# Queries and keys kept as exact float32r halves, attention scores as three products of halves

## The chip, the cores and the metric

The kernel runs on one core of one Trainium2 chip. The metric is the device time of one execution in microseconds (us); what is compared is the median of several executions. The engines are named as the profile names them: PE (TensorE) multiplies, PEld is its loading of weights, DVE is VectorE, ACT is ScalarE, POOL is GpSimd, and SP issues the DMAs that bring the weights in.

## The reference

Two decoder layers over 256 tokens of width 1024, all in float32. Each layer is a half-step SwiGLU, a mixer and a second half-step SwiGLU. The mixer projects once and runs three branches side by side: a gated causal convolution of 31 taps, a gated spatial mixing, and attention with 8 heads of 64. With 256 tokens and blocks of 256 there is one block, so the attention is plain causal attention:

```python
q = _partial_rope(z_q.reshape(bsz, seq, ATT_HEADS, HEAD_DIM), cos, sin)
k = _partial_rope(z_k.reshape(bsz, seq, ATT_HEADS, HEAD_DIM), cos, sin)
...
s = jnp.einsum("bhqd,bhqnkd->bhqnk", qc, kg).astype(jnp.float32) * scale   # scale = 64 ** -0.5
s = jnp.where(mask, s, -jnp.inf)
p = jax.nn.softmax(...)
return jnp.einsum("bhqnk,bhqnkd->bhqd", p, vg)
```

## The kernel before

Weights come in chunks of 1 MB (128 x 2048). Each chunk is split into two float32r halves: ACT copies the rounded half (`whi`, line 114) and DVE subtracts it from the chunk (`wlo`, line 115), in two pieces of 1024 columns in most stages. Activations are split in the same way, and a product of the two is then three matmuls, high by high, low weight by high, high by low (lines 271 to 273, and 456 to 458 in the sections that put tokens on partitions). A chunk is worked on by 48 such matmuls.

The mixer begins with four blocks of the convolution's gate. Then come four sections: queries, keys, the gating's v, the attention's v. `rotated` (464) scales and turns the queries, then the keys. `columns_first` (483) is run in the middle of the next section: PE transposes the turned queries (or keys) so that head dimensions lie on partitions, and ACT copies them to `qT` (or `kT`), with the factor 1/8 for queries. Through all of this DVE has 124 steps of the convolution to do in its free time (`conv`, 438, lines 442 and 444), some after each stage.

After two more blocks (`uT`) comes the stage that the change touches most. `scores(c)` (545) makes the scores of heads 2c and 2c+1, each head in a PSUM bank of its own: a mask product in bf16 (550), a float32 product for the first 128 queries (552) and one for the others (555). DVE takes the maxima (`st`, 565), ACT the exponentials (line 85 in the profile, the helper `act`), DVE divides (570, 572). `turned(c)` (575) transposes them on PE (580) and copies them with ACT (`aT`, 582), `values(c)` (586) multiplies by v (590, 591) and splits the result into `yc_`. The order on PE is: scores(0), scores(1), half a block of gate weights, `mix` (524: the gating's product, 530), half a block; then for c = 0 to 3: turned(c), half a block, values(c), scores(c+2) while there are any, half a block.

All of this shares one group of four PSUM banks, `acc`: the two banks of a scores(c), the two of mix, the two of a turned(c) and the one of a values(c). A tile that finds no free bank waits until an earlier one has been read out for the last time. Likewise `qT`, `kT`, `yc`, `uT`, the halves of the gating (`yb`) and those of the attention's result (`yc_`) share seven places of 4 KB (tag `b4`).

In the trace each engine takes its instructions in the order in which they stand in its queue. That order, and which buffer a tile gets, is set when the program is built: a scheduler goes through the code by priority and by its own estimate of when things are ready. Of an engine's instructions, one that waits holds up all that stand behind it.

Of the kernel before, what the change touches and what calls it, by code (L numbers as in the profile page):

```python
# [9 lines left out]
F32 = mybir.dt.float32  # L10
F32R = mybir.dt.float32r
BF16 = mybir.dt.bfloat16
AF = mybir.ActivationFunctionType
# [4 lines left out]
P = 128  # L18
D = 1024
S = 256  # L20
# [6 lines left out]
NCW = CW // P  # L27
TAPS = 31
HEADS = 8
HD = 64  # L30
# [16 lines left out]
def decoder_kernel(ctx, tc, x_in, wts, rows, lanes, sguw, rope, out):  # L47
    nc = tc.nc
# [8 lines left out]
    sm = ctx.enter_context(tc.tile_pool(name="sm", bufs=4))  # L57
    ps = ctx.enter_context(tc.tile_pool(name="ps", bufs=4, space=PSUM))

    def bank(tag="ps"):  # L60
        return ps.tile([P, 512], F32, name=tag, tag=tag, bufs=4)
# [4 lines left out]
    TS = [slice(t * P, (t + 1) * P) for t in range(NT)]  # L66
# [50 lines left out]
    def cols(n, i):  # L117
        return slice(i * CH // n, (i + 1) * CH // n)
# [11 lines left out]
    def weights():  # L130
        i = used[0]
        used[0] += 1
        ensure(i + LOOK)
        return made.pop(i)
# [128 lines left out]
    def t2(name):  # L263
        return wk.tile([P, 512], F32, name=name, tag="t2", bufs=12)
# [14 lines left out]
    def pair_block(ph, at_k=None, k_at=KD // 2 - 1, nudged=False):  # L279

        w = blocks(KD)
        b = bank()
        if nudged:
            nudge(b, w[0][:, 0, 0], ph.xh)
        for k in range(KD):
            for s in range(2):
                product(b[:, s * S:(s + 1) * S], w, (slice(None), k, s), (ph.xh, ph.xl), k,
                        k == 0 and s == 0, k == KD - 1 and s == 1)
            if at_k is not None and k == k_at:
                at_k()  # L290
        return b

    def scaled(b, ph, name="t"):

        t = t2(name)
        nc.vector.tensor_mul(two(t), two(b), ph.R.to_broadcast([P, 2, S]))  # L296
        return t
# [99 lines left out]
    def wide(name):  # L397
        return mx.tile([P, NCW, S], F32, name=name, tag="b4", bufs=7)

    def halves4(name):  # L400
        return [mx.tile([P, NCW, S], F32R, name=f"y{name}{k}", tag="b4", bufs=7) for k in "hl"]

    def layer_stats(src):
        bs = sm.tile([P, 6], F32, name="bs", bufs=4)
        nc.vector.bn_stats(bs, src)
        mv = sm.tile([P, 2], F32, name="bmv", bufs=4)
        nc.vector.bn_aggr(mv, bs)
        v = sm.tile([P, 1], F32, name="bv", bufs=4)
        nc.vector.tensor_scalar_add(v, mv[:, 1:2], EPS)
        r = sm.tile([P, 1], F32, name="br", bufs=4)  # L410
        nc.gpsimd.tensor_tensor(r, v, mhalf[:, 0:1], op=OP.pow)
        b = sm.tile([P, 1], F32, name="bb", bufs=4)
        nc.vector.scalar_tensor_tensor(b, mv[:, 0:1], -1.0, r, op0=OP.mult, op1=OP.mult)
        return r, b

    def mixer(l, ph, lane, params, make_next):
# [21 lines left out]
        def conv(n, after=None):  # L438
            for k, c in taps[:n]:
                src, w = yp[:, c, k:k + S], convw[:, c, k:k + 1]  # L440
                if k == 0:
                    ins = nc.vector.tensor_scalar(yc[:, c], src, w, cb[:, c:c + 1], op0=OP.mult, op1=OP.add)
                else:
                    ins = nc.vector.scalar_tensor_tensor(yc[:, c], src, w, yc[:, c], op0=OP.mult, op1=OP.add)  # L444
                behind(ins, after)
            del taps[:n]

        def section(between=None):

            b = [bank() for _ in range(NT)]  # L450
            for c in range(2):
                w = [h.rearrange("p (k m) -> p k m", k=4) for h in weights()]
                for t in range(NT):
                    for kk in range(4):
                        hx, lx = (v[:, 4 * c + kk, TS[t]] for v in x)
                        nc.tensor.matmul(b[t], hx, w[0][:, kk], start=c == 0 and kk == 0, stop=False)  # L456
                        nc.tensor.matmul(b[t], hx, w[1][:, kk], start=False, stop=False)  # L457
                        nc.tensor.matmul(b[t], lx, w[0][:, kk], start=False, stop=c == 1 and kk == 3)  # L458
                if c == 0 and between is not None:
                    between()  # L460
            return b


        def rotated(b):
            zs = []
            for t in range(NT):
                zf = t2("zqk")
                nc.scalar.activation(zf, b[t], AF.Identity, scale=ph.r[:, t:t + 1])
                z = zf.rearrange("p (h d) -> p h d", h=HEADS)
                x12 = z[:, :, :RD]  # L470
                sw = sm.tile([P, HEADS, RD], F32, name="sw", bufs=2)
                hf = RD // 2
                cb_ = rp[:, t, 0:1, :].to_broadcast([P, HEADS, RD])
                sb_ = rp[:, t, 1:2, :].to_broadcast([P, HEADS, RD])
                nc.vector.tensor_mul(sw[:, :, :hf], z[:, :, hf:RD], sb_[:, :, :hf])
                nc.vector.tensor_mul(sw[:, :, hf:], z[:, :, :hf], sb_[:, :, hf:])
                nc.vector.tensor_mul(x12, x12, cb_)
                end = nc.vector.tensor_add(x12, x12, sw)
                zs.append(zf)
            conv(11, end)  # L480
            return zs

        def columns_first(dst, srcs, **kw):
            for t in range(NT):
                pt = bank("acc")
                for c in range(NCW):
                    nc.tensor.transpose(pt[:, c * P:(c + 1) * P], srcs[t][:, c * P:(c + 1) * P], ident)
                nc.scalar.activation(dst[:, :, TS[t]], pt.rearrange("p (c m) -> p c m", c=NCW), AF.Copy,
                                     **kw)

        qT, kT = wide("qT"), wide("kT")
        zq = rotated(section())
        zk = rotated(section(lambda: columns_first(qT, zq, scale=HD ** -0.5)))


        b = section(lambda: columns_first(kT, zk))
        gvs = []
        for t in range(NT):
            gv = t2("gv")
            act(gv, b[t], AF.Gelu_apprx_tanh, scale=ph.r[:, t:t + 1])  # L500
            r, b_ = layer_stats(gv)
# [6 lines left out]
        b = section()  # L508
        vt = []
        for t in range(NT):  # L510
            vv = mx.tile([P, HEADS, HD], F32, name=f"v{t}")
            nc.scalar.activation(vv.rearrange("p h d -> p (h d)"), b[t], AF.Identity,
                                 scale=ph.r[:, t:t + 1])
# [4 lines left out]
        for c in (0, 2):  # L518
            t = scaled(pair_block(ph), ph)
# [25 lines left out]
        def scores(c):  # L545
            heads = (0, 1)
            rows_ = [slice(h * HD, (h + 1) * HD) for h in heads]
            pS = [bank("acc") for _ in heads]
            for h in heads:
                nc.tensor.matmul(pS[h][:, :3 * P], ident_b, causal_b, start=True, stop=False)  # L550
            for h in heads:
                nc.tensor.matmul(pS[h][:, 0:P], qT[rows_[h], c, 0:P], kT[rows_[h], c, 0:P],
                                 start=False, stop=False)
            for h in heads:
                nc.tensor.matmul(pS[h][:, P:3 * P], qT[rows_[h], c, P:S], kT[rows_[h], c, :],
                                 start=False, stop=True)
            ways = (slice(0, P), slice(P, 3 * P))
            res = []
            with tc.high_priority():
                for h in heads:  # L560
                    sc = wk.tile([P, 3 * P], F32, name="sc", bufs=4)
                    st = sm.tile([P, NT], F32, name="st", bufs=4)
                    su = sm.tile([P, NT], F32, name="su", bufs=4)
                    for t, w in enumerate(ways):
                        nc.vector.tensor_reduce(st[:, t:t + 1], pS[h][:, w], axis=AX.X, op=OP.max, negate=True)
                    for t, w in enumerate(ways):
                        act(sc[:, w], pS[h][:, w], AF.Exp, bias=st[:, t:t + 1], accum_out=su[:, t:t + 1])
                    res.append((sc, su))
                for sc, su in res:
                    nc.vector.reciprocal(su, su)  # L570
                    for t, w in enumerate(ways):
                        nc.vector.tensor_scalar_mul(sc[:, w], sc[:, w], su[:, t:t + 1])
            return [sc for sc, _ in res]
# [68 lines left out]
        m = [wide("m") for _ in range(2)]  # L642
# [85 lines left out]
    for i in range(2):  # L728
        nc.scalar.dma_start(xt[:, 4 * i:4 * i + 4], x_in[:, 4 * i:4 * i + 4])
        c = cols(2, i)  # L730
        loaded[0] = nc.sync.dma_start(first[0][:, c], wts[0, :, c])
    ph = Phase(lane[0][:, L_GAIN:L_GAIN + KD])
# [25 lines left out]
    for l in range(DEPTH):  # L758
# [3 lines left out]
        def gains(i, cur=cur):  # L762
            return cur[:, L_GAIN + KD * i:L_GAIN + KD * (i + 1)]
# [5 lines left out]
        ph = ffn(ph, lambda: Phase(gains(1)), lambda: params.extend(mixer_params(l)), 2 if l == 0 else 1)  # L769
        ph = mixer(l, ph, cur, params, lambda: Phase(gains(2)))  # L770
        if l < DEPTH - 1:
            ph = ffn(ph, lambda: Phase(lane[-1][:, L_GAIN:L_GAIN + KD]), following)
# [105 lines left out]
```

## Time and profile before

| | us |
|---|---|
| median of 3 runs (lowest to highest) | 1198.89 (1196.75 to 1201.77) |
| the profiled execution, its own time | 1201.76 |
| its span, first to last instruction | 1200.0 |
| PE busy | 1178.3 (98%) |
| DVE busy | 853.8 (71%) |
| ACT busy | 610.5 (51%) |
| PE scores, lines 550 to 555, one call of eight | 1.29 |

Busy shares are means over the whole program; the mixers of the two layers, at about 197 to 417 and 783 to 1003 us, look different from the rest. Durations of matmuls are from first operand in to last result out, so matmuls that follow each other overlap; what one costs is the distance between starts. The same holds in part for DVE: a row `x4` of four instructions takes less than four times one alone.

### The profile page before, as it was taken

The page shows a single profiled execution, that of the slowest core. Times are in us where ns is not written, and L with a number is a line of the kernel's source. Part 1 is how long each engine was busy: PE and PEld are TensorE (multiplying, and loading weights), DVE is VectorE, ACT ScalarE, POOL GpSimd, SP SyncE. Part 2 cuts the span into 40 slices and gives each one's busy share as a digit, 9 for nine tenths or more (in the row PEclk, how much of TensorE's full clock was granted, in tenths as well). Part 3 has the DMA queues.
Part 4 walks back from the last instruction along what each step waited for, and adds up shares of the span by engine and source line. Part 5 has one row for each costly group of instructions (what it writes and reads, how often), then busy time and mean ns, then how long its engine had stood idle before and what let it go on. Part 6 is the DMA issues. An engine that isn't in the chain of part 4 may idle for free.

```text
span 1200.0 us, 22895 instructions
## 1 busy us (share of the span) xinstructions
PE 1178.3 (98%) x9840; PEld 1149.2 (96%) x9840; DVE 853.8 (71%) x1300; ACT 610.5 (51%) x887; POOL 20.2 (2%) x32
## 2 busy tenths in 40 slices
PE   7999999999999999999999999999999999999997
PEld 7999999889999999999999999998889999999997
DVE  6656557699998776556675655677999886656562
ACT  5544445466646554444454444465564565544442
POOL 1000000000000000000000000000000000000000
PEclk9999999999999999999999999999999999999998
DMA  7556555444555545545555565544435545555530
GB/s 290 206 202 219 210 181 182 167 176 141 176 176 178 209 176 178 213 178 209 178 175 204 191 237 180 205 173 147 176 141 176 211 163 189 176 188 198 194 123 36
DMA packets 32069, 219.81 MB, mean 183 GB/s; under 512 B 3680, under 2 KB 3936, under 8 KB 5984
## 3 DMA queue, kind: packets, MB, share of 16 engines
q1 hardware_dynamic: 31248, 216.68, 50.8%
q8 instruction: 77, 1.26, 0.4%
q10 hardware_dynamic: 720, 1.67, 0.4%
q14 instruction: 24, 0.20, 0.0%
HBM read 217.28 MB, written 1.05 MB: 182 GB/s over the span
## 4 chain that ended last, share of the span: by engine, by line
PE 80%; DVE 13%; ACT 3%; DMA 2%; issue 1%; POOL 1%; ACTq 0%; DVEq 0%; POOLq 0%
PE ps L273 17%; PE ps L271 17%; PE ps L272 17%; PE acc L273 7%; PE acc L271 7%; PE acc L272 7%; DVE wlo L115 5%; PE ps L458 2%; PE ps L457 2%; PE ps L456 2%; DVE yc L444 2%; DVE xl L172 1%; ACT whi L114 1%; DMA raw<-wts 1%; DVE x L337 1%
## 5 line engine op out<-in xcount | busy, mean ns | idle before, releaser
L114 ACT ACTIVATE whi<-raw 128x1024 fp32r<-128x1024 f32 (+2 forms) x388 | 418.3, 1098 | 424.7 <-issue 183.1
L115 DVE TENSOR_TENSOR wlo<-raw,whi 128x1024 fp32r<-128x1024 f32 (+2 forms) x388 | 488.7, 1275 | 149.5 <-ACT whi L114 149.4
L271 PE MATMUL ps<-xh,whi 128*128 128x256 f32 x1984 | 552.3, 279 | 3.6 <-ACT whi L114 3.6
L272 PE MATMUL ps<-xh,wlo 128*128 128x256 f32 x1984 | 550.7, 278 | 0.3 <-DVE wlo L115 0.3
L273 PE MATMUL ps<-xl,whi 128*128 128x256 f32 x1984 | 550.1, 278 | 0.5
L271 PEld LDWEIGHTS ps<-xh,whi 128*128 128x128 f32 x1984 | 374.5, 189 | 6.6 <-ACT whi L114 4.1
L273 PEld LDWEIGHTS ps<-xl,whi 128*128 128x128 f32 x1984 | 374.3, 189 | 1.5 <-DVE xl L172 1.5
L272 PEld LDWEIGHTS ps<-xh,wlo 128*128 128x128 f32 x1984 | 374.7, 189 | 0.6 <-DVE wlo L115 0.5
L271 PE MATMUL acc<-hhi,whi 128*128 128x256 f32 x832 | 229.7, 276 | 0.0
L273 PE MATMUL acc<-hlo,whi 128*128 128x256 f32 x832 | 229.7, 276 | 0.0
L272 PE MATMUL acc<-hhi,wlo 128*128 128x256 f32 x832 | 229.6, 276 | 0.0
L296 DVE TENSOR_TENSOR t<-ps,R 128x512 f32<-128x512 f32 x100 | 69.0, 691 | 143.0 <-PE ps L273 133.5
L272 PEld LDWEIGHTS acc<-hhi,wlo 128*128 128x128 f32 x832 | 156.2, 188 | 0.0
L271 PEld LDWEIGHTS acc<-hhi,whi 128*128 128x128 f32 x832 | 156.2, 188 | 0.0
L273 PEld LDWEIGHTS acc<-hlo,whi 128*128 128x128 f32 x832 | 156.2, 188 | 0.0
L444 DVE SCALAR_TENSOR_TENSOR yc<-yp,lane,yc 128x256 f32<-128x256 f32 x240 | 100.1, 477 | 0.0
L141 ACT ACTIVATE hhi<-t 128x256 fp32r<-128x256 f32 x88 | 36.6, 419 | 30.9 <-DVE t L357 30.9
L456 PE MATMUL ps<-whi,xh 128*128 128x512 f32 x128 | 50.3, 393 | 0.0
L458 PE MATMUL ps<-whi,xl 128*128 128x512 f32 x128 | 50.3, 393 | 0.0
L457 PE MATMUL ps<-wlo,xh 128*128 128x512 f32 x128 | 50.1, 392 | 0.0
L85 ACT ACTIVATE t<-t 128x256 f32<-128x256 f32 x96 | 38.6, 403 | 12.5 <-DVE t L296 12.5
L141 DVE TENSOR_TENSOR hlo<-t,hhi 128x256 fp32r<-128x256 f32 x88 | 36.5, 418 | 2.6 <-ACT hhi L141 2.6
(135 smaller groups left out, 837.2 us busy)
## 6 DMA issues: line engine op xcount, KB each, us to landing
raw<-wts SPq DMA_DIRECT2D x203, 1024.0 KB, 4.8
raw<-wts SPq DMA_DIRECT2D x2, 512.0 KB, 5.9
x<-x ACTq DMA_DIRECT2D x2, 512.0 KB, 8.7
wsT<-sguw SPq DMA_DIRECT2D x2, 256.0 KB, 5.2
sgg<-rows SPq DMA_DIRECT2D x2, 256.0 KB, 5.7
sgb<-rows SPq DMA_DIRECT2D x2, 256.0 KB, 5.9
sbr<-rows SPq DMA_DIRECT2D x2, 256.0 KB, 6.8
out<-o SPq DMA_DIRECT2D x2, 256.0 KB, 2.4
```

Source lines behind the costliest of these rows:

```text
L85: ins = nc.scalar.activation(out_, in_, func, **kw)
L114: return (nc.scalar.activation(hi[:, c], raw[:, c], AF.Copy), nc.vector.tensor_sub(lo[:, c], raw[:, c], hi[:, c].bitcast(F32)))
L115: nc.vector.tensor_sub(lo[:, c], raw[:, c], hi[:, c].bitcast(F32)))
L141: return nc.scalar.activation(h, src, AF.Copy), nc.vector.tensor_sub(l, src, h.bitcast(F32))
L271: nc.tensor.matmul(o, w[0][i], x[0][:, k], start=first, stop=False)
L272: nc.tensor.matmul(o, w[1][i], x[0][:, k], start=False, stop=False)
L273: return nc.tensor.matmul(o, w[0][i], x[1][:, k], start=False, stop=last)
L296: nc.vector.tensor_mul(two(t), two(b), ph.R.to_broadcast([P, 2, S]))
L444: ins = nc.vector.scalar_tensor_tensor(yc[:, c], src, w, yc[:, c], op0=OP.mult, op1=OP.add)
L456: nc.tensor.matmul(b[t], hx, w[0][:, kk], start=c == 0 and kk == 0, stop=False)
L457: nc.tensor.matmul(b[t], hx, w[1][:, kk], start=False, stop=False)
L458: nc.tensor.matmul(b[t], lx, w[0][:, kk], start=False, stop=c == 1 and kk == 3)
```

## The change

The turned queries and keys are no longer kept as one float32 tile each but as two float32r halves, as weights and activations are elsewhere. ACT's copy after the transposition now writes the high half, and a new DVE subtraction from PSUM (line 494) writes the low half: four subtractions of 128x512 in a layer. The factor 1/8 moves from that copy to the earlier scaling of the queries, as two DVE products of one column (line 471). A score is then three float32r products, high by high, low query by high key, high query by low key, for the first 128 queries and for the others (lines 558 and 561).

```diff
--- before.py
+++ after.py
@@ -461,11 +461,15 @@
             return b
 
 
-        def rotated(b):
+        def rotated(b, scale=None):
             zs = []
             for t in range(NT):
                 zf = t2("zqk")
-                nc.scalar.activation(zf, b[t], AF.Identity, scale=ph.r[:, t:t + 1])
+                r = ph.r[:, t:t + 1]
+                if scale is not None:
+                    r = sm.tile([P, 1], F32, name="rq", bufs=2)
+                    nc.vector.tensor_scalar_mul(r, ph.r[:, t:t + 1], scale)
+                nc.scalar.activation(zf, b[t], AF.Identity, scale=r)
                 z = zf.rearrange("p (h d) -> p h d", h=HEADS)
                 x12 = z[:, :, :RD]
                 sw = sm.tile([P, HEADS, RD], F32, name="sw", bufs=2)
@@ -480,17 +484,18 @@
             conv(11, end)
             return zs
 
-        def columns_first(dst, srcs, **kw):
+        def columns_first(dst, srcs):
             for t in range(NT):
                 pt = bank("acc")
                 for c in range(NCW):
                     nc.tensor.transpose(pt[:, c * P:(c + 1) * P], srcs[t][:, c * P:(c + 1) * P], ident)
-                nc.scalar.activation(dst[:, :, TS[t]], pt.rearrange("p (c m) -> p c m", c=NCW), AF.Copy,
-                                     **kw)
-
-        qT, kT = wide("qT"), wide("kT")
-        zq = rotated(section())
-        zk = rotated(section(lambda: columns_first(qT, zq, scale=HD ** -0.5)))
+                pv = pt.rearrange("p (c m) -> p c m", c=NCW)
+                nc.scalar.activation(dst[0][:, :, TS[t]], pv, AF.Copy)
+                nc.vector.tensor_sub(dst[1][:, :, TS[t]], pv, dst[0][:, :, TS[t]].bitcast(F32))
+
+        qT, kT = halves4("q"), halves4("k")
+        zq = rotated(section(), HD ** -0.5)
+        zk = rotated(section(lambda: columns_first(qT, zq)))
 
 
         b = section(lambda: columns_first(kT, zk))
@@ -548,12 +553,13 @@
             pS = [bank("acc") for _ in heads]
             for h in heads:
                 nc.tensor.matmul(pS[h][:, :3 * P], ident_b, causal_b, start=True, stop=False)
-            for h in heads:
-                nc.tensor.matmul(pS[h][:, 0:P], qT[rows_[h], c, 0:P], kT[rows_[h], c, 0:P],
-                                 start=False, stop=False)
-            for h in heads:
-                nc.tensor.matmul(pS[h][:, P:3 * P], qT[rows_[h], c, P:S], kT[rows_[h], c, :],
-                                 start=False, stop=True)
+            for i, (a, b) in enumerate(((0, 0), (1, 0), (0, 1))):
+                for h in heads:
+                    nc.tensor.matmul(pS[h][:, 0:P], qT[a][rows_[h], c, 0:P], kT[b][rows_[h], c, 0:P],
+                                     start=False, stop=False)
+                for h in heads:
+                    nc.tensor.matmul(pS[h][:, P:3 * P], qT[a][rows_[h], c, P:S], kT[b][rows_[h], c, :],
+                                     start=False, stop=i == 2)
             ways = (slice(0, P), slice(P, 3 * P))
             res = []
             with tc.high_priority():
```

Queries and keys now take four of the seven `b4` places where they took two, until scores(3) has read them for the last time. The order of PE's other work stays as it was. On PE, the start of the attention stage (scores(0); `qT`, `kT` are the old tiles, `yqh`, `yql`, `ykh`, `ykl` the new halves), before:

```order
L550 MATMUL acc<-causal_b,ident_b 128x384 [waits PE_49]
L552 MATMUL acc<-kT,qT 128x128 x2
L555 MATMUL acc<-kT,qT 128x256 x2
L550 LDWEIGHTS ident_b
L550 MATMUL acc<-causal_b,ident_b 128x384 [waits PE_49]
```

and now:

```order
L555 MATMUL acc<-causal_b,ident_b 128x384 [waits PE_49]
L558 MATMUL acc<-ykh,yqh 128x128 x2
L561 MATMUL acc<-ykh,yqh 128x256 x2
L558 MATMUL acc<-ykh,yql 128x128 x2
L561 MATMUL acc<-ykh,yql 128x256 x2
L558 MATMUL acc<-ykl,yqh 128x128 x2
L561 MATMUL acc<-ykl,yqh 128x256 x2
```

Four products of two heads became twelve.

On DVE, from the last weights before the first maxima to the divisions of the first two pairs of heads (`st` are the maxima, `su` the sums, `sc` the exponentials, `wlo` the low halves of weights, `yc` the convolution), before:

```order
L296 TENSOR_TENSOR t<-ps,R 128x512
L444 SCALAR_TENSOR_TENSOR yc<-yp,lane,yc 128x256
L565 TENSOR_REDUCE st<-acc 128x1 x4
L115 TENSOR_TENSOR wlo<-raw,whi 128x1024
L565 TENSOR_REDUCE st<-acc 128x1 x4
L570 RECIPROCAL su<-su 128x2
L115 TENSOR_TENSOR wlo<-raw,whi 128x1024
L570 RECIPROCAL su<-su 128x2
L572 TENSOR_SCALAR sc<-sc,su 128x128 x2
```

and now:

```order
L296 TENSOR_TENSOR t<-ps,R 128x512
L444 SCALAR_TENSOR_TENSOR yc<-yp,lane,yc 128x256
L115 TENSOR_TENSOR wlo<-raw,whi 128x1024
L571 TENSOR_REDUCE st<-acc 128x1 x4
L115 TENSOR_TENSOR wlo<-raw,whi 128x1024
L571 TENSOR_REDUCE st<-acc 128x1 x4
L576 RECIPROCAL su<-su 128x2
L444 SCALAR_TENSOR_TENSOR yc<-yp,lane,yc 128x256
L576 RECIPROCAL su<-su 128x2
L578 TENSOR_SCALAR sc<-sc,su 128x128 x2
```

A piece of weights that stood behind the first maxima stands ahead of them now, and the one that stood behind the second maxima stands between the two.

On DVE again, a little later, from the end of the gating (`ybl`) to the maxima of scores(2), before:

```order
L539 TENSOR_TENSOR zb<-zb,uT 128x256
L296 TENSOR_TENSOR gate<-ps,R 128x512
L444 SCALAR_TENSOR_TENSOR yc<-yp,lane,yc 128x256
L141 TENSOR_TENSOR ybl<-zb,ybh 128x256
L444 SCALAR_TENSOR_TENSOR yc<-yp,lane,yc 128x256 x2
L115 TENSOR_TENSOR wlo<-raw,whi 128x1024 x2
L565 TENSOR_REDUCE st<-acc 128x1 x4
```

and now:

```order
L544 TENSOR_TENSOR zb<-zb,uT 128x256 x2
L444 SCALAR_TENSOR_TENSOR yc<-yp,lane,yc 128x256
L141 TENSOR_TENSOR ybl<-zb,ybh 128x256 x4
L296 TENSOR_TENSOR gate<-ps,R 128x512
L115 TENSOR_TENSOR wlo<-raw,whi 128x1024 x2
L444 SCALAR_TENSOR_TENSOR yc<-yp,lane,yc 128x256 x3
L115 TENSOR_TENSOR wlo<-raw,whi 128x1024 x2
L571 TENSOR_REDUCE st<-acc 128x1 x4
```

All four `ybl` come after the last use of `uT`, and four pieces of weights, not two, stand in a row ahead of the maxima of scores(2). Both layers have this same order.

## Rows read from the trace of the kernel before

**Rows 1.** The page's busy time of each engine over the span.
```profile
PE 1178.3 (98%) x9840; PEld 1149.2 (96%) x9840; DVE 853.8 (71%) x1300; ACT 610.5 (51%) x887; POOL 20.2 (2%) x32
```

**Rows 2.** Busy time by stretch; then TensorE's granted clock, DMA share, GB/s.
```profile
203.00:213.00 10.00, 8.88 (x76) 8.68 (x75) 6.67 (x11) 5.45 (x8) 1.60 (x1) 1.00 0.60 212
258.80:296.80 38.00, 38.00 (x289) 34.01 (x289) 37.97 (x88) 22.43 (x44) 1.51 (x1) 1.00 0.37 130
297.20:363.60 66.40, 66.06 (x575) 63.99 (x574) 66.29 (x117) 36.56 (x55) 0.20 (x1) 1.00 0.52 183
```

**Rows 3.** Timeline of PE at scores(0): start, duration, line, tiles, count, idle before.
```profile
278.47 0.28 PE L272 MATMUL ps<-xh,wlo 128*128 128x256 f32 x1
278.58 0.28 PE L273 MATMUL ps<-xl,whi 128*128 128x256 f32 x1
...
279.13 0.49 PE L552 MATMUL acc<-kT,qT 64*128 64x128 f32 x4
...
279.45 0.39 PE L555 MATMUL acc<-kT,qT 64*128 64x256 f32 x2
...
279.67 0.38 PE L555 MATMUL acc<-kT,qT 64*128 64x256 f32 x2
...
279.99 0.50 PE L550 MATMUL acc<-causal_b,ident_b 128*128 128x384 bf16 x2
```

**Rows 4.** Timeline of DVE from the keys' section to scores(3), first layer.
```profile
245.85 0.23 DVE L475 TENSOR_TENSOR sw<-zqk,rp 128x64 f32<-128x64 f32 x1 [1.34 <-ACT zqk L468]
...
251.14 4.62 DVE L115 TENSOR_TENSOR wlo<-raw,whi 128x1024 fp32r<-128x1024 f32 x4
255.68 0.68 DVE L405 BATCH_NORM_STATS2 bs<-gv 128x6 f32<-128x512 f32 x1
...
257.43 0.16 DVE L413 SCALAR_TENSOR_TENSOR bb<-bmv,br 128x1 f32<-128x1 f32 x1 [0.66 <-POOL br L411]
...
263.66 7.61 DVE L444 SCALAR_TENSOR_TENSOR yc<-yp,lane,yc 128x256 f32<-128x256 f32 x19
...
279.89 0.69 DVE L296 TENSOR_TENSOR t<-ps,R 128x512 f32<-128x512 f32 x1
...
280.89 1.15 DVE L565 TENSOR_REDUCE st<-acc 128x1 f32<-128x128 f32 x4
...
284.14 0.15 DVE L570 RECIPROCAL su<-su 128x2 f32<-128x2 f32 x1
...
295.42 1.14 DVE L565 TENSOR_REDUCE st<-acc 128x1 f32<-128x128 f32 x4
...
304.85 1.15 DVE L565 TENSOR_REDUCE st<-acc 128x1 f32<-128x128 f32 x4
```

**Rows 5.** Timeline of ACT: exponentials of scores(0) to (3), and the copy `aT` of turned(2).
```profile
283.24 0.47 ACT L85 ACTIVATE sc<-acc,st 128x256 f32<-128x256 f32 x1
...
284.37 0.49 ACT L85 ACTIVATE sc<-acc,st 128x256 f32<-128x256 f32 x1
...
296.51 0.47 ACT L85 ACTIVATE sc<-acc,st 128x256 f32<-128x256 f32 x1
...
305.93 0.47 ACT L85 ACTIVATE sc<-acc,st 128x256 f32<-128x256 f32 x1
...
309.02 0.86 ACT L582 ACTIVATE aT<-acc 128x384 f32<-128x384 f32 x2
```

**Rows 6.** Timeline of PE at mix, turned(1), turned(2), values(2), first layer.
```profile
284.11 2.05 PE L530 MATMUL acc<-wsT,gv 128*128 128x128 f32 x16
...
297.21 0.82 PE L580 MATMUL acc<-ident,sc 128*128 128x128 f32 x6
...
305.64 0.82 PE L580 MATMUL acc<-ident,sc 128*128 128x128 f32 x6
...
309.54 0.81 PE L590 MATMUL acc<-aT,v 128*64 128x256 f32 x3 [0.34 <-ACT aT L582]
```

**Rows 7.** Timeline of PE at mix, second layer.
```profile
870.46 2.31 PE L530 MATMUL acc<-wsT,gv 128*128 128x128 f32 x16 [0.41 <-ACT sc L85]
```

## The prediction

> **What bounds the kernel now.** I read the page's busy line first, then a table of busy time by stretch, then the timelines of PE, DVE and ACT through the first mixer. The page says that PE is busy 98% of the span and DVE 71% [rows 1]. Over the whole program PE is the bound, and a change that saved PE time would show almost in full. The table by stretch says something else of the attention: from 258.8 to 296.8 us DVE is busy 37.97 of 38.00 us, and from 297.2 to 363.6 us 66.29 of 66.40 [rows 2]. There two engines are full at once. PE is never short of work, yet what DVE owes it comes late. The first maxima begin at 280.89 although scores(0) was through by 279.99 [rows 3, 4]; DVE was still at a `t` of 0.60 us and a convolution step of 0.40. PE begins mix at 284.11, and mix waits for the bank that the exponential of 283.24 leaves at 283.71 [rows 5, 6]. So it has 0.40 us to spare. The second half of turned(1) starts three of six transpositions after 297.21, at 297.54, and its bank is left by the exponential of 296.51 at 296.98: 0.56 to spare. At values(2) PE already waits, for ACT's `aT` [rows 6]. My question for the change is therefore what it puts on DVE ahead of the maxima.
>
> **The change part by part.** *PE's products.* Now, scores(0) takes 0.32 us for the 128-query products and 0.54 for the others, with the gap to the next mask product [rows 3]: 0.86, and 6.9 over eight calls. The two heads run side by side: a float32 product leaves two records, and of the four of 256 columns two start together at 279.45 and two at 279.67, 0.22 us on, while float32r products of 256 columns start 0.11 us apart [rows 3]. New: six rounds of two heads. The trace has no float32r product on 64 rows, nor one of 128 columns. If heads still go side by side and every round costs what the 256-column product costs, the sum is 6 x 0.11 and, for the first weights and the gap, about 0.2: 0.86, no change. If the 128-column rounds cost half, it is 0.17 less; if the heads go one after the other, 12 x 0.11 + 0.2 = 1.5, or 0.66 more. I take no change, as the nearest row says. None of this reaches the end time while the steps below hold: the maxima that follow are late by DVE's queue, not by PE.
>
> The Trainium skill says that loading weights takes columns/1.2 ns whatever the number of rows ("TensorE: Matmul & The Clock Gate", LDWEIGHTS): 107 ns for 128 columns, so that a 128-column product would be bound by its load. By that a round is never under 0.107 us, and the calls are worth nothing either way, as in the value that I take.
>
> *Scaling the queries.* Two products of one column on DVE fall into its pauses near 208 us, where it is busy 6.67 of 10 us [rows 2]. Nothing. ACT's copies keep their size and count.
>
> *Subtractions.* Four of 128x512 from PSUM, per layer. The like of it is `t`: from 279.89 to 280.89, less one convolution step of (7.61 - 0.48)/18 = 0.40, is 0.60 us [rows 4]. The two for the queries (1.2) stand before the second turn of the keys, for which DVE waits 1.34 us [rows 4]: hidden. The two for the keys stand in the middle of the four pieces of weights at 251.14. There the only pause is the 0.66 for POOL and 0.13 behind it [rows 4]; the new order puts the second statistics into it, which hides 0.45 to 0.8. So 0.4 to 1.2 us stay, and I take 0.75.
>
> *Order before the first maxima.* One piece of weights now stands ahead of them. Four pieces take 251.14 to 255.68, so one takes 1.14 [rows 4]. The first maxima come 0.75 + 1.14 = 1.9 us later, and with them the table load and the exponentials. PE's mix, with 0.4 to spare, waits 1.5. Its second half, 0.89 later at 285.00, had 0.14 to spare against the exponential that ends at 284.86 [rows 5, 6]; it is 1.8 late in all. First charge: 1.8.
>
> *Order before the maxima of scores(2).* Between the divisions at 284.14 and the maxima at 295.42 DVE works 11.28 us [rows 4]. The new order has one more piece of weights there (1.14; four for three) and three more convolution steps (6 for 3; 1.19), and about 0.35 of waiting for exponentials that used to be covered. The maxima come 1.9 + 2.7 = 4.6 late. PE is only 1.8 late, plus 0.1 at values(0), where `aT` now stands behind all four `ybh` and a piece of weights. So the second half of turned(1), with 0.56 to spare, is 4.6 - 0.56 = 4.05 late. Second charge: 2.15 more. What is queued on PE behind this wait is all its work.
>
> *Order before the maxima of scores(3).* Between 295.42 and 304.85 there are three more convolution steps, but one piece of weights and two `ycl` of 0.34 less, and 0.2 of waiting is gone: 0.65 shorter. These maxima come 3.95 late, and the exponential that ended at 306.40 [rows 5] ends at 310.35. Before, the first half of turned(2) did not wait for it; in the new program the values' results stay in their banks until scores(3) is through, since `ych` and `ycl` now get the places of the queries and keys, and turned(2) takes the bank of the first head of scores(3). It wanted to start at 305.64 + 4.05 = 309.7 [rows 6], and starts at 310.4: 4.7 late.
>
> *What is given back.* values(2) began at 309.54, after 0.34 of waiting for `aT` [rows 6]. `aT` hangs on the exponentials, 3.95 late, so its second copy ends at 309.88 + 3.95 = 313.85 [rows 5]; PE arrives at 309.2 + 4.7 = 313.9. The old wait is gone: 313.9 for 309.54, or 4.3 us in the first layer. Afterwards DVE has fewer steps left than before (nine extra convolution steps are done, 3.6 us), and it reached its next pause at 363.6 [rows 2]; I cost the rest of the mixer at nothing.
>
> *Second layer.* It has the same order. But its mix already waits 0.41 us at 870.46, for the exponentials [rows 7], where the first layer's has 0.4 to spare. The lateness of ACT that this shows does not add to that of the maxima, since both hold up the same exponentials. The first layer's 4.3 is then too much by between 0.41 and 0.8; I charge 4.3 - 0.6 = 3.7.
>
> *Sum.* 4.3 + 3.7 = 8.0 us. The profiled execution took 1201.76, so its like would take 1209.8; the median is 2.9 lower, and the forecast is 1198.9 + 8.0 = 1206.9 us.
>
> **Rivals.** *A, the delay is covered.* DVE could be late with the maxima and PE not: if the keys' subtractions vanish in the pause (0.4 left) and the exponentials gain on ACT. For it: the queries' subtractions do vanish. Against it: DVE has 0.03 us of pauses in 38 [rows 2], and PE's spare times are 0.4, 0.14 and 0.56 us. With the order's own 1.14 and 2.7 halved, 2 us per layer would be left: 1203. With all covered, 1199.
>
> *B, not slower: the products decide.* Three single-pass products could beat two records of float32. The price is bounded by what scores cost, 0.17 x 8 = 1.4 us from the shorter rounds, so 1197.5. It decides only where the maxima wait for PE; here they wait for DVE by 0.9 us [rows 3, 4], and by 1.9 to 4.6 more in the new order. So B needs DVE's lateness to vanish as well.
>
> The Trainium skill says that true FP32 takes four passes ("FP8 and Floating Point Precision", TensorE Precision Notes). By it three passes would cost three quarters, some 1.5 us less over eight calls, an estimate that gives the same 1197.4 as B. The rows agree with four: each of a float32 product's two records takes 0.22 us, twice a float32r product of that width [rows 3].
>
> *C, slower: the banks decide.* The results of values(0) and values(1) now hold two of four banks until scores(3) is through. turned(2)'s second half waits for the first `ycl`, values(2) for the second, which stands behind a reciprocal. By my times the second ends near 310.9, and values(2) comes at 313.9: 3 us to spare. If DVE were over 3 us later than I think, each layer would lose that excess, say 1.5: 1210.
>
> *D, slower: the clock.* PE would pause 1.5, 2.2 and 0.7 us. If a pause cost the clock, half a block of 24 products at 0.11 would take 2.7 us longer, four times: 1218. Against it: around the wait near 208, where PE is busy 8.88 of 10 us, the granted clock is 1.00 [rows 2].
>
> **How the numbers follow.** Forecast 0.68, A 0.20, B 0.03, C 0.06, D 0.03. The forecast's own range is 1203 to 1211: 0.4 to 1.2 for the keys' subtractions is 0.7 us in two layers, reciprocals and copies whose waits I only estimated are 1 us in each, and the measured runs lie up to 2.9 us from their median. With most of A and C it is 1199.5 to 1211. What this measurement can tell from no change is about 0.5%, or 6 us, so slower means over 1204.9. Of the forecast 0.75 lies above that, C and D do wholly, of A a tenth: 0.62 slower. B and the lowest of A give 0.03 faster, the rest is 0.35.
>
> **What would show it.** Right: new PE waits at mix (about 1.5 us, for exponentials), in the middle of turned(1) (2.2) and at the start of turned(2) (0.7), none left at values(2), in both layers; maxima of scores(0), (2) and (3) later against PE's order by 1.9, 4.6 and 4.0 us; four subtractions near 0.7 us; DVE full from the keys to 363 us. The six rounds of a scores call take about 0.86 us. Wrong: PE without waits there; maxima on time; a scores call much over 1.5 us, which could reach past DVE's delay; or weights (`wlo`) late for a chunk, which I cost at nothing.

## The result and the profile after

The changed kernel takes 1208.7 us, median of 4 runs (1207.99 to 1210.0), against 1198.58 us (1196.75 to 1201.77) for the kernel before, 10.1 us more. The ratio on record, which is not that of the two medians, is 1.0077, with a 95% interval of 1.0061 to 1.0093, or 7.3 to 11.1 us. Forecast were 1206.9 us and 8.0 more. The execution that was profiled took 1210.0 us, its span is 1208.3.

The page's busy line answers to [rows 1]: PE is as full as before, and DVE has 12 instructions more.

```profile
PE 1181.7 (98%) x9872; PEld 1154.1 (96%) x9872; DVE 859.2 (71%) x1312; ACT 610.2 (51%) x887; POOL 20.0 (2%) x32
```

What PE waited for, over the whole program (line waited at, releaser, us in all, how often, the longest):

```profile
PE acc L586 <- ACT sc L85: 4.0, 2, 2.0
PE acc L535 <- ACT sc L85: 3.0, 2, 1.5
```

Line 586 is a transposition of `turned`, line 535 the product of `mix`. Neither stands in the list of the kernel before with more than 0.4, and the 0.6 us that it waited for `aT` at values(2) are gone. The same on PE's timeline, first layer, beside [rows 6]:

```profile
284.13 2.31 PE L535 MATMUL acc<-wsT,gv 128*128 128x128 f32 x16 [1.53 <-ACT sc L85]
...
297.61 0.49 PE L586 MATMUL acc<-ident,sc 128*128 128x128 f32 x3
...
300.12 0.55 PE L586 MATMUL acc<-ident,sc 128*128 128x128 f32 x3 [2.02 <-ACT sc L85]
...
309.93 0.82 PE L586 MATMUL acc<-ident,sc 128*128 128x128 f32 x6
...
313.42 0.66 PE L596 MATMUL acc<-aT,v 128*64 128x256 f32 x4
```

The second layer has the same two waits, at 877.51 (1.52) and 893.50 (2.02). DVE's maxima, beside [rows 4]:

```profile
281.18 1.14 DVE L571 TENSOR_REDUCE st<-acc 128x1 f32<-128x128 f32 x4
...
298.42 1.15 DVE L571 TENSOR_REDUCE st<-acc 128x1 f32<-128x128 f32 x4
...
307.19 1.15 DVE L571 TENSOR_REDUCE st<-acc 128x1 f32<-128x128 f32 x4
```

In this execution PE reached scores(0) 1.74 us sooner than in the other (277.39 for 279.13), in the main because the clock of the other fell in the first SwiGLU (told below). Against PE the maxima of scores(0), (2) and (3) are thus 2.03, 4.74 and 4.08 us late. The row that I had not expected is the granted clock (the seventh number behind the stretch is PEclk; before it, us, and busy time of PE, PEld, DVE, ACT, POOL):

```profile
300.20:305.20 5.00, 5.00 (x29) 4.83 (x31) 5.00 (x12) 3.33 (x8) 0.00 (x0) 0.66 0.44 185
893.50:898.50 5.00, 5.00 (x29) 4.80 (x31) 5.00 (x12) 3.40 (x8) 0.00 (x0) 0.66 0.47 190
```

Behind the wait in turned(1), in both layers, PE is busy 5.00 of 5.00 us and does 29 products. The same stretch of the kernel before has 46, at a clock of 1.00:

```profile
297.60:302.60 5.00, 5.00 (x46) 4.11 (x44) 5.00 (x13) 3.32 (x7) 0.00 (x0) 1.00 0.42 177
```

PE's clock fell to the lower of its two levels, 1.2 GHz, for part of the stretch: from 301.03 to 304.24 its products start 0.21 us apart, not 0.11.

**Where the 10 us are.** I matched PE's products of the two traces and measured each mixer from the last product ahead of scores(0) to the eleventh of the convolution's branch (`yah`; 384.97 before, 388.56 now). The first mixer takes 5.3 us longer, the second 4.6: 9.9 in all. The span grew by 8.3, since the stages outside the mixers differ too, in the main by falls of the same clock that come and go from one execution to the next. Outside the mixers and apart from the first and last microseconds, there are two in the profiled execution of before, at the waits that end at 28.7 and 1014.9; in that of after there is one, near 800.

### The profile page after: what moved, and what is told of

Read it like the earlier page. It is cut to its first block, busy times and chain, and to the rows that moved or that the text cites. A ratio compares the mean times of both kernels' runs of the same rounds, so it can differ in the third digit from the quotient of the medians.

```text
span 1208.3 us, 22971 instructions
## 1 busy us (share of the span) xinstructions
PE 1181.7 (98%) x9872; PEld 1154.1 (96%) x9872; DVE 859.2 (71%) x1312; ACT 610.2 (51%) x887; POOL 20.0 (2%) x32
## 4 chain that ended last, share of the span: by engine, by line
PE 78%; DVE 15%; ACT 2%; DMA 1%; issue 1%; POOL 1%; ACTq 0%; DVEq 0%; POOLq 0%
PE ps L271 17%; PE ps L272 17%; PE ps L273 17%; PE acc L271 7%; PE acc L273 7%; PE acc L272 7%; DVE wlo L115 6%; DVE yc L444 3%; DVE xl L172 1%; PE ps L458 1%; PE ps L457 1%; PE ps L456 1%; ACT whi L114 1%; DVE x L337 1%; DMA x<-x 1%
## 5 line engine op out<-in xcount | busy, mean ns | idle before, releaser
L357 DVE TENSOR_TENSOR t<-t 128x256 f32<-128x256 f32 x88 | 36.8, 419 | 1.7 <-ACT t L85 1.4
```

Source lines behind the costliest of these rows:

```text
L357: nc.vector.tensor_mul(g, g, t[:, S:])
```

## Experiments

In the table a mixer's delay is measured in that way against the profiled execution of before; the waits are those of PE, first and second layer, in us. Ratios are of several executions; delays, waits and falls of the clock are those of the one execution of each kernel that was traced.

| kernel | ratio to before (95%) | delay of mixers | wait at mix | wait in turned(1) | clock falls in attention |
|---|---|---|---|---|---|
| the change | 1.0077 (1.0061 to 1.0093) | 5.3, 4.6 | 1.5, 1.5 | 2.0, 2.0 | both layers |
| the change, again | 1.0092 (1.0075 to 1.0109) | 5.3, 3.7 | 1.5, 1.5 | 2.0, 2.0 | first only |
| change, fewer steps ahead of maxima | 0.9990 (0.9977 to 1.0003) | -0.2, -0.7 | none | none | none |
| the same, again | 0.9992 (0.9981 to 1.0004) | -0.2, -0.4 | 0, 0.3 | none | none |
| before, fewer steps | 0.9998 (0.9988 to 1.0008) | -0.5, -1.0 | none | none | none |
| change, mix late only | 1.0036 (1.0022 to 1.0050) | 1.6, 0.9 | 1.8, 1.8 | none | none |
| change, turned(1) late only | 1.0056 (1.0044 to 1.0068) | 4.2, 3.5 | 0.2, 0.2 | 2.2, 2.2 | both |
| change, turned(1) less late | 1.0025 (1.0015 to 1.0035) | 1.8, 1.0 | none | 1.8, 1.8 | none |
| change, one product | 0.9999 (0.9984 to 1.0014) | -0.2, 0.7 | 1.9, 1.9 | none | second, behind mix |
| change, nine places | 1.0076 (1.0052 to 1.0100) | 4.0, 3.4 | 1.5, 1.5 | none (1.4 at values(2)) | none |
| before, dummy work ahead of maxima | 1.0086 (1.0065 to 1.0107) | 5.1, 4.4 | 1.4, 1.4 | none | none |

**Fewer steps ahead of the maxima.** The theory: PE's waits come from what stands ahead of the maxima in DVE's queue. The rivals: the three products, the places of the halves, or DVE's added work as such. All of the change stays in this kernel; convolution steps move.

```diff
-        conv(14, end)
+        conv(9, end)
...
-            conv(5)
+            conv(2, end)
...
+        held = [None]
...
-                        nc.vector.tensor_reduce(st[:, t:t + 1], ...)
+                        held[0] = nc.vector.tensor_reduce(st[:, t:t + 1], ...)
...
-            conv(3)                     # and the later conv(...) in the same way
+            conv(3, held[0])
```

> The changed kernel, with 11 convolution steps fewer on DVE ahead of the first maxima and the later steps held behind the maxima that stand before them in the program; nothing is left out, the steps are done later. By the order on DVE the maxima of scores(0) now stand 0.94 us earlier than in the kernel before, less the keys' subtractions (0.75), and those of scores(2) 2.1 earlier, less the same. Theory (DVE is late with the maxima): no PE wait at mix in the first layer, at most 0.4 in the second, none in the middle of turned(1), no fall of the granted clock at 0.5 behind it; 1197.5 to 1199.5 us, a ratio of 0.999 to 1.001. Rival, the three products or the places of the halves cost the time: unchanged, 1207 to 1210. Rival, the added work on DVE as such: it comes back as a wait where the convolution is handed to PE, 1203 or more.

It took 1198.69 us beside 1200.48 for the kernel before. PE's list of waits has no line of `mix`, `turned` or `values` left, and mix and turned(1) run through:

```profile
282.44 2.27 PE L535 MATMUL acc<-wsT,gv 128*128 128x128 f32 x16
...
295.92 0.82 PE L588 MATMUL acc<-ident,sc 128*128 128x128 f32 x6
...
304.38 0.82 PE L588 MATMUL acc<-ident,sc 128*128 128x128 f32 x6
```

The order of PE's instructions is that of the changed kernel, and products, copies, subtractions and places are all there. The whole loss is gone, so none of these is its cause by itself. It is the order on DVE.

**What the change costs without the waits.** The same rule in the kernel before (the edit is the same, on the old code), and the kernel with fewer steps once more, on one chip.

> The kernel before, with float32 scores, and the same rule for the convolution as in the kernel with fewer steps ahead of the maxima (11 steps fewer, the later ones held behind the maxima); by the order on DVE its maxima are 0.9 and 2.1 us earlier than in the kernel before. It asks what the change itself costs once the maxima wait for nothing in either. Theory: no wait at mix, turned or values(2); 0.3 to 1.2 us under the kernel before, a ratio of 0.999 to 1.000, and no more than 0.5 us from the changed kernel with fewer steps. Rival, the change costs or saves PE time that the waits hid: the two differ by more than 2 us.

> The changed kernel with fewer steps ahead of the maxima once more, beside it on the same chip. Theory: 0.998 to 1.000 of the kernel before, no waits in the attention, and within 0.5 us of the kernel before with the same rule.

1199.55 and 1199.82 us, beside 1200.14 for the kernel before. The two differ by 0.3 us, less than the interval of either (1.2 and 1.4 us each way); the change costs PE nothing that these runs can tell. Neither is clearly faster than the kernel before.

**Mix alone, turned(1) alone.** Here I put the lateness back in two portions, with PE's order unchanged. `behind(x, y)` makes the instruction x stand behind y. For mix alone: `conv(9, end)`, `conv(5, end)` and `conv(0, held[0])` in the edit above. For turned(1): `conv(9, end)`, `conv(3, end)`, and twelve steps ahead of the maxima of scores(2). The smaller dose has `conv(2, end)` and eleven.

```diff
+            last = conv(12, held[0]) if c == 2 else None
...
-                        held[0] = nc.vector.tensor_reduce(st[:, t:t + 1], ...)
+                        held[0] = behind(nc.vector.tensor_reduce(st[:, t:t + 1], ...), last)
```

> The changed kernel with the steps ordered so that the first maxima are late as in it (by the order on DVE 1.44 us, with the keys' subtractions 2.2) and those of scores(2) are not (0.9 early); PE's order is that of the changed kernel, and nothing is left out. Theory (each late maximum costs what PE waits for it, and the fall of the clock comes with the second wait alone): PE waits 1.5 to 1.9 at mix in both layers, none in the middle of turned(1), no granted clock of 0.5 in the attention; 3 us over the kernel with fewer steps, a ratio of 1.001 to 1.002. Rival, any wait of 1.5 us costs the clock: 6 us more, 1.004. Rival, the products: as the changed kernel, 1.008.

> The changed kernel with the first maxima nearly on time (by the order and the keys' subtractions 0.6 us late) and twelve convolution steps ahead of the maxima of scores(2), which are 3.1 late; PE's order is that of the changed kernel, nothing is left out. Theory: PE waits 0.2 at mix in the first layer and 0.6 in the second, 2.0 to 2.6 in the middle of turned(1), and the clock falls to 0.5 for 3.4 us behind that; about 8 us over the kernel with fewer steps, a ratio of 1.005 to 1.006. Rival, the fall of the clock in the changed kernel was chance: no fall, 5 us more, 1.003. Rival, it is the sum of mix and turned(1) that matters: no wait left in turned(1), 1.001.

> The same with the first maxima on time (0.2 early) and eleven steps ahead of the maxima of scores(2), one piece of weights fewer: these are 1.9 us late. Theory: no wait at mix in the first layer, 1.2 to 1.5 in the middle of turned(1). Waits of 1.5 in the changed kernel did not cost the clock, so none falls here: 2.5 to 3 us over the kernel with fewer steps, a ratio of 1.001 to 1.002. Rival, the clock falls behind any wait in turned(1): 6 more, 1.004.

PE's timeline of the kernel with mix late only, first layer, and then its busy time and clock in the five us behind the wait:

```profile
284.21 2.31 PE L535 MATMUL acc<-wsT,gv 128*128 128x128 f32 x16 [1.81 <-ACT sc L85]
```

```profile
284.20:289.20 5.00, 4.99 (x41) 4.81 (x42) 4.71 (x20) 2.98 (x14) 0.00 (x0) 1.00 0.59 210
```

The same two views of the kernel with turned(1) late only:

```profile
298.43 0.55 PE L591 MATMUL acc<-ident,sc 128*128 128x128 f32 x3 [2.18 <-ACT sc L85]
```

```profile
298.40:303.40 5.00, 4.97 (x29) 4.84 (x31) 4.99 (x12) 3.44 (x8) 0.00 (x0) 0.66 0.11 18
```

And with turned(1) less late:

```profile
298.11 0.55 PE L591 MATMUL acc<-ident,sc 128*128 128x128 f32 x3 [1.78 <-ACT sc L85]
```

```profile
298.10:303.10 5.00, 4.99 (x45) 4.24 (x45) 5.00 (x12) 3.43 (x8) 0.00 (x0) 1.00 0.11 13
```

Where the clock fell, PE did 29 products in the five us behind turned(1); where it held, 45.

Against the kernel with fewer steps, the mixers grew by 1.8 and 1.7 us for a wait of 1.8 at mix, and by 2.0 and 1.7 for one of 1.8 in turned(1): a wait costs about its length. With 2.2 and 0.2 they grew by 4.4 and 4.2: 1.8 to 2.0 us over the waits, of which a fall of the clock takes about 1.6 (read from two traces below). From the smaller dose to the larger there are 0.6 us more of waiting and 2.4 more of time. For the smaller dose I had expected a wait of 1.2 to 1.5 and 1.001 to 1.002; it waited 1.8 and came out at 1.0025, with the rival's 1.004 outside the interval. For mix alone it is the other way round: the interval of 1.0022 to 1.0050 leaves out the theory's 1.001 to 1.002 and holds the rival's 1.004. In the execution that was traced the clock held, but it was the fastest of six (1201.84 us); one other took 1201.94, the remaining four 1204.45 to 1206.72. The mean granted clock of those four is 0.993, that of the two 0.995, so falls of the clock may be in them, perhaps behind mix; without their traces this is open.

**The changed kernel again.**

> The changed kernel itself once more, for a second trace. Theory: the same waits (1.5 at mix, 2.0 in the middle of turned(1), none at values(2)) and again a granted clock of 0.5 for 3.4 us behind the second of them in both layers; 1207 to 1210. Rival, the clock's fall is chance: it stands elsewhere, or in one layer only.

Its two executions took 1211.36 and 1211.80 us, above the 1207 to 1210 expected, with 1200.38 for the kernel before beside them. The waits came again, within 0.02 us. The fall came in the first layer and not in the second:

```profile
301.90:306.90 5.00, 4.99 (x29) 4.86 (x31) 5.00 (x12) 3.41 (x8) 0.00 (x0) 0.66 0.46 188
893.90:898.90 5.00, 5.00 (x45) 4.25 (x47) 5.00 (x12) 3.40 (x8) 0.00 (x0) 1.00 0.47 192
```

So it is neither certain nor rare. Where the clock held, the next wait of the forecast shows up, at turned(2):

```profile
902.58 0.88 PE L586 MATMUL acc<-ident,sc 128*128 128x128 f32 x6 [0.34 <-ACT sc L85]
```

The second mixer is then 3.7 us longer, where it was 4.6 with the fall.

**One product.** `for i, (a, b) in ((2, (0, 0)),)` in place of the three rounds.

> The changed kernel with the product of the high halves alone (the two with low halves are left out, so the scores are rounded); the four subtractions and the seven places stay. The order on DVE changes with it: no piece of weights ahead of the first maxima, so that they are late by the subtractions alone (0.4 to 0.8 us), those of scores(2) by less. Theory: PE waits 0.4 at mix in the first layer and 0.8 in the second and nowhere else in the attention; a scores call takes 0.4 to 0.5 us less, eight of them 3 to 4; 1195 to 1197. Rival, the products alone: three rounds cost more than the 0.03 us a call that the trace shows, then this is the faster by as much, under 1195. Rival, the places: waits at turned(2) or values(2) stay, 1200 or more.

1200.09 us beside 1200.48, not 1195 to 1197. The rival of the places had 1200 or more, but with waits at turned(2) or values(2), and there are none. A call of scores takes 0.86 us (277.14 to 278.00, mask product to mask product) for 1.32, so the price of the two other rounds is as expected. But PE waits 1.94 us at mix, in both layers:

```profile
283.80 1.16 PE L535 MATMUL acc<-wsT,gv 128*128 128x128 f32 x8 [1.94 <-ACT sc L85]
```

I had forgotten that PE comes to mix 0.9 us earlier when two calls are shorter, while the maxima follow DVE's queue: they start at 280.22, still 0.9 late against PE. What PE saves ahead of a wait is lost in it. In the second layer the clock fell behind this wait of 1.94; in the first it held behind one of the same length.

```profile
869.00:874.00 5.00, 4.92 (x28) 4.84 (x29) 4.87 (x18) 2.86 (x14) 0.00 (x0) 0.66 0.50 165
```

**Nine places.** `bufs=9` for the tag `b4`; 10 for 12 of `t2`, 3 for 4 of `t1`, for the room.

> The changed kernel with nine places of 4 KB for seven, so that the gating's low half and the halves of the attention's result wait for no earlier tile (the room comes from two of twelve 2 KB tiles and one of four 1 KB tiles). The order on DVE keeps the piece of weights ahead of the first maxima and drops one of the two added ahead of those of scores(2), which are then 1.1 less late and 0.3 later by one more copy. Theory: mix waits 1.5 as in the changed kernel, the middle of turned(1) 1.2 for 2.0; 1206.5 to 1207.5 if the clock still falls behind that wait, 1203 to 1204.5 if it doesn't. Rival, the places cost the time: 1198 to 1200. Rival, the products: 1208 to 1210.

1209.54 us, 1.0076. That is what the rival of the products expected, which the kernel with fewer steps has ruled out. Of the theory only the wait of 1.5 at mix came. The wait in turned(1), 1.2 by the theory, is gone altogether; the clock holds in the attention, for which the theory had 1203 to 1204.5; and a wait comes back at values(2):

```profile
313.01 0.81 PE L596 MATMUL acc<-aT,v 128*64 128x256 f32 x3 [1.38 <-ACT aT L588]
```

The maxima of scores(3) start at 308.34, 3.93 late against PE (which reached scores(0) 0.44 sooner here), ACT loads its table behind the exponentials (1.28 us), and `aT` follows that. I had followed the lateness to turned(1) and not on to the next maxima. So nine places do not bring the time back; what changed is at which of the waits DVE's lateness is paid. The convolution is handed over late as well, with waits of 0.64 and 0.70 us. The traced execution has mixers of 4.0 and 3.4 us more and a fall of the clock near 616, outside them.

**Dummy work in the kernel before.**

```diff
+                late_ = None
+                for _ in range({0: 4, 2: 10}.get(c, 0)):
+                    d = t2("dummy")
+                    late_ = behind(nc.vector.tensor_sub(d, gvs[0], gvs[1]), late_)
```

with each maximum put behind `late_`.

> The kernel before, whole, with dummy subtractions of 128x512 on DVE ahead of the maxima: four for scores(0), ten for scores(2). By the order on DVE (some pieces of weights and steps fall behind the maxima in exchange) the maxima are 2.0 and 4.6 us late, as in the changed kernel (2.0 and 4.7); the float32 scores, the places and the copies are those of before. Theory: PE waits about 1.5 at mix and 2 in the middle of turned(1) in both layers, the clock falls to 0.5 for some 3.4 us behind the second wait, and the time is 1207 to 1211. Rival, the products, the subtractions or the places cost the time: 1198 to 1200.

1210.79 us, as the theory has it, but not by its path: PE waits 1.4 at mix, none in turned(1) (the scheduler put PE's work into another order there), and then 2.7 us where the convolution is handed over. I put that down to the dummies, 14 subtractions a layer that DVE never gets back:

```profile
380.46 0.33 PE L695 MATMUL acc<-ident,zn 128*128 128x128 f32 x1 [0.22 <-ACT zn L688]
381.72 0.98 PE L695 MATMUL acc<-ident,zn 128*128 128x128 f32 x7 [0.92 <-ACT zn L688]
...
387.12 0.40 PE L277 MATMUL ps<-yah,whi 128*128 128x288 f32 x1 [1.58 <-ACT yah L141]
```

The agreement proves little. The kernels that move steps and keep PE's order carry the proof.

## Why the prediction was right, step by step

- **Products: right.** A call takes 1.32 us for 1.29 [rows 3], 0.03 more. The loads of weights (PEld) tell why it is no less:

```profile
277.50 0.19 PEld L561 LDWEIGHTS acc<-ykh,yqh 64*128 64x128 f32 x2
277.61 0.19 PEld L558 LDWEIGHTS acc<-ykh,yql 64*128 64x128 f32 x2
277.73 0.19 PEld L561 LDWEIGHTS acc<-ykh,yql 64*128 64x128 f32 x2
```

  The two heads load side by side, and each round starts 0.11 us behind the last, whether it has 128 columns or 256. The Trainium skill's rule ("TensorE: Matmul & The Clock Gate", LDWEIGHTS), columns/1.2 ns or 107 ns a load, agrees with these 0.11.
- **Subtractions: right.** Two take 1.28 us together, 0.60 each by their distance. Those of the queries vanish: DVE's wait of 1.34 ahead of the second turn [rows 4] is 0.25 now. Those of the keys and all else left the first maxima 0.89 later than the piece of weights (1.14) explains, where I took 0.75.

```profile
239.51 1.28 DVE L494 TENSOR_TENSOR yql<-acc,yqh 128x512 fp32r<-128x512 f32 x2
...
244.12 0.23 DVE L479 TENSOR_TENSOR sw<-zqk,rp 128x64 f32<-128x64 f32 x1 [0.25 <-ACT zqk L472]
```

- **Maxima: right, with a slip.** 2.03, 4.74 and 4.08 us late, forecast 1.9, 4.6 and 3.95. The parts given for scores(3) (three steps more at 0.40, a piece of 1.14 and two `ycl` of 0.34 less, 0.2 of waiting less) add up to 0.83 less, not 0.65, which would make it 3.8.
- **Mix and turned(1): right.** Waits of 1.53 and 2.02, forecast 1.5 and 2.15, in both layers; and the wait of before at values(2) is gone.
- **The clock: wrong.** This is rival D, which I gave 0.03 and 2.7 us four times. It came behind turned(1) alone, in both layers of one trace and in one layer of another. Its price is read from the second mixers of these two traces: from ahead of the wait to the half block that follows scores(3), PE's lag to its matched products of before grew by 3.9 us with the fall (7.21 to 11.07) and by 2.3 without (7.60 to 9.87), so 1.6. I had dismissed it by one wait near 208, of 1.12 us, behind which the clock held [rows 2]. The same trace had the counter-examples, at two longer waits for the same tile (1.60 and 1.30 us), and I did not look there:

```profile
28.00:33.00 5.00, 4.30 (x24) 4.30 (x25) 3.60 (x5) 2.50 (x4) 0.65 (x1) 0.66 0.81 339
1014.00:1020.00 6.00, 5.06 (x30) 5.06 (x31) 1.78 (x4) 2.12 (x4) 0.89 (x1) 0.72 0.69 258
```

  The Trainium skill ("TensorE: Matmul & The Clock Gate", Part 1) says that how busy PE has been of late sets its clock; that agrees with falls that come behind waits.
- **turned(2): right in kind, covered.** The 0.65 us did not show where the clock had fallen, because PE came later; where it held, 0.34 did.
- **DVE full to 363 us: not quite.** Its first pause now ends at 359.54, and the first one before at 364.83. It has fewer steps left there, as the prediction says:

```profile
359.54 2.29 DVE L115 TENSOR_TENSOR wlo<-raw,whi 128x2048 fp32r<-128x2048 f32 x1 [1.04 <-ACT whi L114]
```

- **The sum.** First mixer: forecast 4.3, plus 1.6 for the clock, less 0.65 at turned(2), is 5.25; measured 5.3. Second mixer: forecast 3.7, measured 3.7 where the clock held and 4.6 where it fell. In the traced execution the mixers' 9.9 for 8.0 is thus the 1.6 of the clock in each layer, less the 0.65 that turned(2) did not cost. That the median's 10.1 is made up in the same way is not shown, as the other three executions were not traced. The median stays inside 1203 to 1211 because the range had room left for other reasons, the subtractions, the copies and the spread of the runs. In that part the agreement is luck.

Rival A (covered) and B (products) are out by the waits. C (the banks) is out for this order: values(2) starts without a wait.

## What to carry to other kernels

Read what a change adds on an engine together with what the new order puts ahead of the instruction that others wait for: here, by the order on DVE, four subtractions cost under a microsecond a layer, and pieces of weights and convolution steps that changed places with the maxima cost the rest. An edit that gets lost in one engine's order can be repaired there: holding work that isn't urgent behind the urgent instruction brought all of the 10 us back, with every product of the change in place. And a new pause of PE of about 2 us can cost more than itself (behind six of the eight from 1.94 to 2.18 us the clock fell), so a trace should be searched for what the clock did behind all pauses of that length, not behind one.

## What the runs showed of the hardware

In the traced executions the clock held, in the attention, behind all ten waits of 1.4 to 1.5 us and all four of 1.8. It fell behind one of two of 1.94, behind three of four of 2.02, and behind both of 2.18. A fall cost about 1.6 us. Waits of 1.3 to 1.8 us at the start of the SwiGLUs had it in some executions and not in others, so length alone does not decide.

At a granted clock of 1.00 PE's products start 0.113 us apart in most stretches and 0.118 in some. In the profiled execution of the change the slower spacing lasts from 386 to 430 us and costs 1.1 us. Nothing in the trace says why.
